# Which loads go around one DMA engine: two of q in place of three of k

## The chip, the core, the metric

One NeuronCore of a Trainium2 chip; the time is the device time of one execution in microseconds (us). A ratio is the mean time of one kernel's runs over the mean of the other's from the same rounds on the same chip, so it is not quite the ratio of the medians quoted beside it.

## The reference

Rotary embedding of q and k, then all scores per head. Everything is float32.

```python
# batch, seq, heads, dim = 16, 512, 16, 64
q_rot = concat([q1*cos - q2*sin, q1*sin + q2*cos], -1)      # k_rot likewise
scores = einsum('bshd,bthd->bsht', q_rot, k_rot)            # (16, 512, 16, 512)
```

It reads 2 x 33.6 MB and writes 268.4 MB. Any kernel for it moves 336 MB.

## The kernel before

The work runs in 64 steps of 128 rows of one batch (16 batches x 4). In each step TensorE makes 16 score blocks, ScalarE (ACT) copies them from PSUM into one of three 4 MB stage buffers, and SyncE (SP) stores the stage. VectorE (DVE) makes the rotary embedding, TensorE transposes. All loads and stores of q, k and the scores are issued by SP and stand in one queue (q1 on the page: 16992 packets, 329.65 of the 335.87 MB), in the order of their issue (a q load issued at 135.40 us behind three stores has its packets from 156 us), except for the loads named in `RELIEVED`:

```python
RELIEVED = {("k", 5): 0, ("k", 9): 1, ("k", 13): 2}     # (tensor, batch): number
SLOW = 4

def load(which, b):
    ...                                                  # buffers: two of q, two of k, by b % 2
    if (which, b) not in RELIEVED:
        dma(SP, ..., dram[which][b], sem, writes=rows + rest)          # 2 MB, 128 rows
        return
    n, E, F = 120, C * H * D, C * H * D // 2
    x = RELIEVED[which, b]
    plan.add(POOL, None, (), rows)                       # wait until the buffer is free, then
                                                         # reset the cursor of GpSimd's DMAs
    ...                                                  # 5 tiny rows (SLOW + 1) ahead of the load
    dma(POOL, nc.gpsimd, dst, src, "cursor", ...)
    ...                                                  # rows 0..119, each in two halves of 8 KB
    dma(POOL, nc.gpsimd, dst, src, f"part{x}", writes=rows)
    dma(SP, nc.sync, t[n:]..., d[n:], sem, writes=rest)  # rows 120..127
```

In the trace of this kernel each relieved load is 240 packets of 8 KB, 16 (8 rows) on each of 15 of the 16 sequences of packets; the sequence left out is the slow one. With six tiny rows in place of five (around5 below) another one was left out, one that stores at 1213 ns elsewhere. No record carries the number of an engine: the engine left out with five tiny rows is called engine 4 here. The loop over steps ends with

```python
    if i % C == C - 2:
        load("q", i // C + 2)     # in SP's order: behind the store of this step
    elif i % C == C - 1:
        load("k", i // C + 3)
```

Of the kernel before, what the change touches and what calls it, by code (L numbers as in the profile page):

```python
# [178 lines left out]
def kernel(  # L179
# [56 lines left out]
    def dma(engine, e, dst, src, sem, reads=(), writes=(), also=()):  # L236
        plan.add(engine, one(lambda: e.dma_start(dst, src)), reads, writes, sem=sem, also=also)  # L237
# [19 lines left out]
            writes=[("unit", which, u) for u in us], also=[x for u in us for x in unit_keys(which, u)],  # L257
        )

    RELIEVED = {("k", 5): 0, ("k", 9): 1, ("k", 13): 2}  # L260
    SLOW = 4

    def load(which, b):
# [5 lines left out]
        rest = [("in rest", which, b % 2, c) for c in range(C)]  # L269
        if (which, b) not in RELIEVED:  # L270
            dma(SP, nc.sync, t.rearrange("p c (h d) -> p c h d", h=H), dram[which][b], sem, writes=rows + rest)
# [4 lines left out]
        n, E, F = 120, C * H * D, C * H * D // 2  # L276
        x = RELIEVED[which, b]
        plan.add(POOL, None, (), rows)
# [252 lines left out]
```

## Time and profile before

| | before |
|---|---|
| median of its runs | 806.99 us (804.74 to 807.4) |
| span of the profiled run | 803.3 us |
| DMA queues busy | 97.0% + 2.3% |
| PE, ACT, DVE busy | 85%, 70%, 68% |

The page's first part and its account of the DMA issues (tensor moved, issuing engine, count, KB each, median us from issue to landing) show the parties. The lines that carry the argument stand in the prediction below.

```profile
PE 680.6 (85%) x3072; PEld 295.1 (37%) x3072; DVE 544.8 (68%) x516; ACT 562.1 (70%) x647; POOL 4.8 (1%) x12
...
out_dram<-st SPq DMA_DIRECT2D x60, 4096.0 KB, 24.7
q_sb<-in_q_dram SPq DMA_DIRECT2D x15, 2048.0 KB, 27.6
k_sb<-in_k_dram SPq DMA_DIRECT2D x12, 2048.0 KB, 27.1
...
k_sb<-in_k_dram POOLq DMA_DIRECT2D x3, 1920.0 KB, 29.8
```

A 4 MB store moves in 9.7 us (128 packets of 1213 ns over 16 engines) and lands 24.7 us after its issue (the median of 60), so as a rule two or more stand in the queue.

Some words for what follows. q1 is the DMA queue of SP, q0 that of GpSimd. A relief is one load that goes around the slow engine. A deal is the way in which the rows of a transfer are shared out over the engines. A packet is stretched when it takes longer than its nominal time, the one that most packets of its size show (in the kernel before, within 6 ns, 1213 ns for 7180 of 7680 stores of 32 KB and 611 for 2937 of 3480 reads of 16 KB).

### The profile page before, as it was taken

How to read it: one execution, taken by the hardware profiler on the slowest of the kernel's cores; microseconds unless marked ns; L12 is line 12 of the kernel's file. 1: busy time of each engine (PE TensorE's matmuls, PEld its weight loads, DVE VectorE, ACT ScalarE, POOL GpSimd, SP SyncE). 2: the span in 40 equal slices, each digit the busy share in tenths (PEclk: the TensorE clock that was granted, in tenths of full speed). 3: DMA queues.
4: the chain of work that ended last, by engine and by line, in shares of the span. 5: the costliest groups of instructions: out<-in, count | busy, mean ns of one | idle time of the engine just before them, and what ended most of it. 6: DMA issues, size and time to landing. Idle time of an engine off the chain costs nothing.

```text
span 803.3 us, 8192 instructions
## 1 busy us (share of the span) xinstructions
PE 680.6 (85%) x3072; PEld 295.1 (37%) x3072; DVE 544.8 (68%) x516; ACT 562.1 (70%) x647; POOL 4.8 (1%) x12
## 2 busy tenths in 40 slices
PE   4989998968989979795897997979499799799960
PEld 2444443423433334242343443434244344343420
DVE  6999987665866767575686675858478568586400
ACT  3878886757858758673785886768388578578770
POOL 0000000000000000000000000000000000000000
PEclk9999999898999989998899899989889889899995
DMA  8999999999999999999999999999999999999996
GB/s 342 425 423 426 433 425 433 401 370 430 434 433 426 439 429 431 433 381 374 434 429 432 430 432 436 428 437 368 401 423 433 431 433 435 432 435 429 434 432 295
DMA packets 18209, 335.87 MB, mean 418 GB/s; under 512 B 1960, under 2 KB 3240, under 8 KB 4264
## 3 DMA queue, kind: packets, MB, share of 16 engines
q1 hardware_dynamic: 16992, 329.65, 97.0%
q0 software_dynamic: 912, 5.90, 2.3%
q10 hardware_dynamic: 288, 0.13, 0.1%
q8 instruction: 6, 0.10, 0.0%
q14 instruction: 11, 0.09, 0.0%
HBM read 67.24 MB, written 268.44 MB: 418 GB/s over the span
## 4 chain that ended last, share of the span: by engine, by line
DMA 48%; PE 35%; DVE 8%; ACT 5%; issue 1%; ACTq 0%; DVEq 0%; SPq 0%
DMA out_dram<-st 47%; PE ps L393 27%; PE bank L344 9%; ACT st L402 5%; DVE st L319 3%; DVE part L319 2%; DVE k_sb L319 2%; DVE q_sb L319 1%; DMA st<-in_k_dram 1%; DVE kT L362 0%; DVE qT L362 0%; ACTq L110 0%; DVEq L110 0%; SPq L526 0%; SPq L497 0%
## 5 line engine op out<-in xcount | busy, mean ns | idle before, releaser
L402 ACT COPY st<-ps 128x1024 f32<-128x1024 f32 x512 | 495.2, 1018 | 203.6 <-DMA out_dram<-st 109.2
L393 PE MATMUL ps<-kT,qT 64*128 64x512 f32 x2048 | 539.1, 643 | 81.8 <-ACT st L402 81.7
L393 PEld LDWEIGHTS ps<-kT,qT 64*128 64x128 f32 x2048 | 181.7, 194 | 268.7 <-issue 135.1
L362 DVE COPY qT<-bank 128x512 f32<-128x512 f32 x118 | 81.5, 690 | 197.4 <-PE bank L344 197.4
L344 PEld LDWEIGHTS bank<-ident,q_sb 128*128 128x128 f32 x480 | 54.7, 150 | 101.6 <-issue 97.3
L344 PE MATMUL bank<-ident,q_sb 128*128 128x128 f32 x480 | 85.5, 305 | 1.0 <-DVE q_sb L319 1.0
L344 PEld LDWEIGHTS bank<-ident,k_sb 128*128 128x128 f32 x480 | 50.5, 141 | 93.3 <-DVE k_sb L319 44.4
L319 DVE TENSOR_TENSOR part<-q_sb,ss_t 128x1024 f32<-128x1024 f32 x60 | 73.5, 1224 | 10.3 <-DMA q_sb<-in_q_dram 7.6
L344 PE MATMUL bank<-ident,k_sb 128*128 128x128 f32 x480 | 78.7, 287 | 1.6 <-DVE qT L362 0.8
L362 ACT COPY kT<-bank 128x512 f32<-128x512 f32 x122 | 72.6, 598 | 6.7 <-PE bank L344 6.7
L319 DVE TENSOR_TENSOR k_sb<-k_sb,cos_t 128x1024 f32<-128x1024 f32 x60 | 73.5, 1225 | 2.0
L319 DVE TENSOR_TENSOR q_sb<-q_sb,cos_t 128x1024 f32<-128x1024 f32 x60 | 73.5, 1225 | 2.1
L319 DVE TENSOR_TENSOR k_sb<-k_sb,part 128x1024 f32<-128x1024 f32 x60 | 73.5, 1225 | 2.1
L319 DVE TENSOR_TENSOR part<-k_sb,ss_t 128x1024 f32<-128x1024 f32 x60 | 72.9, 1215 | 0.3
L319 DVE TENSOR_TENSOR q_sb<-q_sb,part 128x1024 f32<-128x1024 f32 x60 | 72.9, 1215 | 0.0
L344 PE MATMUL bank<-ident,st 128*128 128x128 f32 x64 | 10.8, 318 | 13.0 <-DVE st L319 12.9
L344 PEld LDWEIGHTS bank<-ident,st 128*128 128x128 f32 x64 | 8.2, 161 | 18.4 <-DVE st L319 16.6
L319 DVE TENSOR_TENSOR part<-st,ss_t 128x1024 f32<-128x1024 f32 x8 | 9.8, 1222 | 6.1 <-DMA st<-in_k_dram 5.7
L319 DVE TENSOR_TENSOR st<-st,part 128x512 f32<-128x512 f32 x16 | 11.0, 690 | 0.5
L319 DVE TENSOR_TENSOR st<-st,cos_t 128x1024 f32<-128x1024 f32 x8 | 9.8, 1225 | 0.3
L362 ACT COPY qT<-bank 128x512 f32<-128x512 f32 x10 | 5.7, 617 | 3.5 <-PE bank L344 3.5
L237 POOL DMA_DIRECT2D scratch<-in_q_dram x3 | 1.8, 616 | 543.2 <-PE bank L344 543.2
(11 smaller groups left out, 9.1 us busy)
## 6 DMA issues: line engine op xcount, KB each, us to landing
out_dram<-st SPq DMA_DIRECT2D x60, 4096.0 KB, 24.7
q_sb<-in_q_dram SPq DMA_DIRECT2D x15, 2048.0 KB, 27.6
k_sb<-in_k_dram SPq DMA_DIRECT2D x12, 2048.0 KB, 27.1
out_dram<-st SPq DMA_DIRECT2D x16, 1024.0 KB, 13.7
k_sb<-in_k_dram POOLq DMA_DIRECT2D x3, 1920.0 KB, 29.8
st<-in_k_dram SPq DMA_DIRECT2D x1, 1536.0 KB, 8.9
st<-in_q_dram SPq DMA_DIRECT2D x1, 1536.0 KB, 12.1
st<-in_k_dram SPq DMA_DIRECT2D x1, 512.0 KB, 4.7
```

Source lines behind the costliest of these rows:

```text
L237: plan.add(engine, one(lambda: e.dma_start(dst, src)), reads, writes, sem=sem, also=also)
L319: plan.add(DVE, one(lambda: nc.vector.tensor_tensor(o, a, b, op=op)), reads, writes, also=more)
L344: done = [nc.tensor.transpose(bank[:, x, :], srcs[x], ident) for x in range(4)]
L362: plan.add(engine, one(lambda: copy(out=dst, in_=src)), [("bank", m)], keys)
L393: nc.tensor.matmul(out=ps[:, r, :], lhsT=lhs[lo:hi, :], rhs=rhs[lo:hi, :], start=True, stop=True)
L402: plan.add(ACT, one(lambda: nc.scalar.copy(out=so, in_=si)), [("ps", y)], [("st", s, p)])
```

## The change

Its intent: relieve engine 4 with loads of q, which become free to start at another moment, and with two instead of three.

```diff
-    RELIEVED = {("k", 5): 0, ("k", 9): 1, ("k", 13): 2}
+    RELIEVED = {("q", 6): 0, ("q", 12): 1}
```

## The prediction

> **What bounds the kernel now.** I read first the page's rows by slice, then its DMA queues, then the chain of waits, then stretches of time, then the single packets of the trace. Slices, queues and chain, from the page:
>
> ```profile
> DMA  8999999999999999999999999999999999999996
> GB/s 342 425 423 426 433 425 433 401 370 430 434 433 426 439 429 431 433 381 374 434 429 432 430 432 436 428 437 368 401 423 433 431 433 435 432 435 429 434 432 295
> ...
> q1 hardware_dynamic: 16992, 329.65, 97.0%
> q0 software_dynamic: 912, 5.90, 2.3%
> ...
> DMA 48%; PE 35%; DVE 8%; ACT 5%; issue 1%; ACTq 0%; DVEq 0%; SPq 0%
> DMA out_dram<-st 47%; PE ps L393 27%; PE bank L344 9%; ACT st L402 5%; DVE st L319 3%; DVE part L319 2%; DVE k_sb L319 2%; DVE q_sb L319 1%; DMA st<-in_k_dram 1%; DVE kT L362 0%; DVE qT L362 0%; ACTq L110 0%; DVEq L110 0%; SPq L526 0%; SPq L497 0%
> ```
>
> The DMA row is full in all inner slices, and the longest single item of the chain is a store of the output. PE is 85% busy, but waits for stage buffers that stores hold. So the bytes bound it: 335.87 MB. A 32 KB store packet takes 1213 ns (7180 of 7680 packets are within 6 ns of that), so 16 engines at full pace move 432 GB/s. The GB/s row is there in most slices and falls in three places, slices 7-8, 17-18 and 27-28 of 20 us. Stretches inside these dips and beside them (us, busy time of the engines, granted clock, DMA share, GB/s):
>
> ```profile
> 120.00:150.00 30.00, 26.26 (x114) 11.21 (x112) 21.50 (x21) 20.82 (x25) 0.00 (x0) 0.89 0.99 427
> 157.00:167.00 10.00, 10.00 (x52) 4.41 (x50) 8.53 (x9) 8.69 (x10) 0.00 (x0) 1.00 1.01 280
> 170.00:178.00 8.00, 4.60 (x22) 1.79 (x20) 4.59 (x5) 2.15 (x3) 0.00 (x0) 0.97 1.01 431
> 355.00:366.00 11.00, 11.00 (x54) 4.63 (x50) 9.53 (x9) 9.31 (x11) 0.00 (x0) 1.00 1.00 268
> 555.00:566.00 11.00, 11.00 (x56) 5.15 (x56) 9.49 (x10) 9.67 (x12) 0.00 (x0) 1.00 1.02 282
> ```
>
> Packets are always in flight (share 1.0), but at 157-167 they move 280 GB/s. What runs there is told by the issues, GpSimd's and SyncE's:
>
> ```profile
> 150.37 0.68 POOL L237 DMA_DIRECT2D scratch<-in_q_dram  x1 [148.85 <-PE bank L344]
> 151.04 0.75 POOL L237 DMA_DIRECT2D k_sb<-in_k_dram  x1
> 348.52 0.58 POOL L237 DMA_DIRECT2D scratch<-in_q_dram  x1 [196.73 <-PE bank L344]
> 349.11 0.75 POOL L237 DMA_DIRECT2D k_sb<-in_k_dram  x1
> ```
> ```profile
> 114.98 20.37 SPq L237 DMA_DIRECT2D out_dram<-st  x3
> 135.40 0.90 SPq L237 DMA_DIRECT2D q_sb<-in_q_dram  x1
> 151.76 0.33 SPq L237 DMA_DIRECT2D out_dram<-st  x1
> ```
>
> The GpSimd load of k (q0) has packets from 156.4 to 178.3 us. The q load that SyncE issued at 135.4 stands in q1 behind three stores and has its 16 KB packets from 156 to 169. Where both loads run, packets stretch: q's from 611 ns to about 1000, q0's 8 KB ones from 309 to about 500. From 170 on q0 runs beside stores and both are at their nominal 309 and 1213. So **a load beside a load costs; a load beside a store does not.** Time over nominal of all packets, divided by 16, is 4.25, 5.04 and 4.68 us for the three relieved loads: 14.0 of 16.6 us in the whole run.
>
> **The slow engine.** Packet records carry no engine number, but following each packet from the end of the one before gives 16 sequences. In one of them the store packets take 1250 ns (427 such packets, evenly spread from 80 to 781 us) and 16 KB reads 620-625: 3% slow. In the windows I followed it is just this sequence that has no q0 packets. So the detour works on the right engine. Its reads beside the k loads stretch too: eight took 8.26 us in the first window and 8.35 in the third, against 5.0 at its own pace, +3.3 us each.
>
> [...] 240 8 KB packets per load, 16 on each of 15 sequences, none on the slow one. [...] 1213, 309, 1213, 309 in a sequence. [...] Here there is one slow sequence, and it is slow long before and after any software DMA. [...]
>
> **The change part by part.** The order of instructions of PE, DVE and ACT is the same in both programs; GpSimd issues two relieved loads in place of three, SyncE's entries keep their places with other sizes. The bytes are the same.
>
> *Removed: three k loads by q0.* The stretch goes: 14.0 us for the mean engine, 3 x 3.3 = 9.9 us for the slow one.
>
> *Added: two q loads by q0. Do they meet another load?* The k buffer comes free at the transposes near a step's end, 10 us after the step's stage buffer landed (139.9 to 150.2), when an SP load of q is just coming up. The q buffer comes free at the second q transpose in the middle of a step. For batch 6 that is step 18: the store that it waits for lands at 227.06, the transposes end at 230.8. q0's first data came 5.4 us after its issue (151.04 to 156.41), so here at about 237. The SP load before it, k of batch 6, stands directly behind that store in q1 and landed on all engines between 227.6 and 231.9. The next one, k of batch 7, stands behind four more stores (9.7 us each), after 275; q0 takes some 24 us beside stores (16 packets of 309, each after a 1213), so it is over by 262. Clear by 5 us in front and over 10 behind. Batch 12 repeats it 24 steps later. Cost of the stretch: near 0 (q0 beside stores: about 0.1 us).
>
> *Moved: bytes of the slow engine.* A relieved load spares it seven of eight 16 KB reads (one of the remaining eight rows is its own): 7 x 0.625 = 4.4 us. Three become two: +4.4 us. [...]
>
> *Sum.* Slow engine: last packet now 798.1, minus 9.9, plus 4.4 = 792.6. The others: mean end now 797.6, the latest 800.7; minus about 14 gives 784 to 787. So the end passes to the slow engine and comes 800.7 - 792.6 = 8.1 us earlier. Time: 806.99 - 8.1 = 798.9, about **799 us** (-1.0%).
>
> **Rivals.** *A: the q loads meet a load after all* (descriptors late, or the order in q1 shifts). Then two stretches stay: slow engine 798.1 - 3.3 + 4.4 = 799.2, the others 800.7 - 4.7; the time is about 805. For it: 5 us is not much. Against: both ends of the gap hang on the same landing, so they shift together. *B: the slow engine matters less without the profiler.* Then the others set the end, near 787: time about 793. Against: the run with profile took 805.04, among the plain ones. *C: the slow engine's lag blocks the stage buffers.* It grows 1.4 us a batch (32 store packets of 37 ns and 16 reads of some 12 ns over nominal): from about 1 us at 75 us, ten batches less the first relief's 4.4 make some 10 us before batch 12; a store lives 22 to 28 us in q1, so it starves only engines that are ahead anyway, not itself. If worse, some us. *D: the change only undoes relief:* with the stretch taken as harmless it is +4.4, 811. Against: the dips in GB/s, and batches with a relieved k load: k issues lie 52.0 and 54.2 us apart across these, about 48.4 elsewhere. *E: another bound.* PE, ACT and DVE keep their order and wait for stores now; no speed below 790 comes from them.
>
> **Range and chances.** Main line 799, A 805, B 793, D 811: 8 in 10 for 794 to 804.5. Faster by over 2% needs less than 790.9, less than B gives: 0.03. Slower by over 2% needs 823: nothing seen leads there, 0.02. Within 2%: 0.95.
>
> **What would show it.** In the changed profile: no dips near 360 and 560, at most small ones near 235-262 and 525-555; the packets there at 309 beside 1213; total time over nominal near 3 us per engine, not 16.6; the span near 795; the last store's sixteen arrivals with one straggler about 5 us or more behind the rest, where now they spread evenly over 6.7 us; GpSimd's two issues some 4 us after a store lands. It is wrong if a 16 KB read of 1000 ns stands beside q0 (A), if the last arrivals bunch (B), or if DMA's share falls below 0.97 in the middle (C).

## The result, and the profile after

| | before | after |
|---|---|---|
| median of its runs (beside each other) | 805.91 us (n 4) | 801.61 us (n 4, 801.0 to 802.06) |
| span of the profiled run | 803.3 us | 799.2 us |
| ratio, 95% interval | | 0.9945 (0.9923 to 0.9967) |

It is 0.55% faster, within 2%, and inside the range of 794 to 804.5; the point, 799 or -1.0%, was 2.6 us too low. The gain was about half of the 8.1 us that the sum gave: 4.4 us by the ratio. The page of the changed kernel, slices, queues and chain:

```profile
DMA  8999999999999999999999999999999999999994
GB/s 346 421 422 424 428 432 427 427 436 430 431 428 431 411 431 426 439 430 433 432 426 433 431 427 431 431 425 420 430 426 436 433 429 434 431 434 403 441 423 180
...
q1 hardware_dynamic: 17120, 331.62, 97.3%
q0 software_dynamic: 608, 3.93, 1.2%
...
DMA 47%; PE 36%; DVE 8%; ACT 6%; issue 1%; ACTq 0%; DVEq 0%; SPq 0%
```

The three dips are gone (370, 374 and 368 GB/s before). The same stretches of time as before, and the two in which the q loads run (columns as in the prediction; the last is GB/s):

```profile
157.00:167.00 10.00, 10.00 (x50) 4.43 (x48) 8.53 (x9) 8.67 (x11) 0.00 (x0) 1.00 1.02 433
230.00:262.00 32.00, 28.64 (x122) 11.90 (x120) 20.98 (x20) 22.07 (x26) 0.00 (x0) 0.89 1.01 429
522.00:556.00 34.00, 29.94 (x120) 12.41 (x120) 20.30 (x20) 23.49 (x27) 1.33 (x2) 0.85 1.01 423
355.00:366.00 11.00, 11.00 (x53) 4.68 (x52) 9.49 (x10) 9.67 (x12) 0.00 (x0) 1.00 1.01 435
```

433 where it was 280, 435 where it was 268, and 429 and 423 beside the new GpSimd loads. Those loads are issued as foreseen, in the timeline of GpSimd, and between two SP loads, in that of SyncE:

```profile
228.14 0.69 POOL L237 DMA_DIRECT2D scratch<-in_q_dram  x1 [226.62 <-PE bank L344]
228.82 0.75 POOL L237 DMA_DIRECT2D q_sb<-in_q_dram  x1
526.51 0.58 POOL L237 DMA_DIRECT2D scratch<-in_q_dram  x1 [296.94 <-PE bank L344]
527.09 0.75 POOL L237 DMA_DIRECT2D q_sb<-in_q_dram  x1
```
```profile
201.07 1.03 SPq L237 DMA_DIRECT2D k_sb<-in_k_dram  x1
210.72 24.33 SPq L237 DMA_DIRECT2D out_dram<-st  x3
235.09 1.12 SPq L237 DMA_DIRECT2D q_sb<-in_q_dram  x1
251.17 0.35 SPq L237 DMA_DIRECT2D out_dram<-st  x1
251.56 1.38 SPq L237 DMA_DIRECT2D k_sb<-in_k_dram  x1
```

The k load issued at 201.07 had landed by 228.85; q0's packets run from 234.5 to 257.2; the next k load came after. Nothing overlaps here. In the second window six 16 KB reads, of the eight rows that SP loads itself, ran beside the last 5 us of q0, at 612 to 968 ns. The end is told by the sixteen arrivals of the last store, one from each engine (from the records of its semaphore, us):

```
          first    median   15th     last
before    794.28   798.11   800.48   801.01
after     787.06   787.20   790.01   796.96
```

Before, the arrivals spread over 6.7 us; after, fifteen end 11 us earlier at the median and one straggles by 7. That it is the slow engine shows in its pace: the straggler's last nine stores arrive at 718.04, 727.99, 737.98, 747.94, 757.88, 767.79, 777.61, 787.28 and 796.96, that is 9.8 to 10.0 us each (about 1250 ns a packet) up to about 777 and 9.68 after.

### The profile page after: what moved, and what is told of

The parts are those of the page before. It is cut to its first block, busy times and chain, and to the rows that moved or that the text cites.

```text
span 799.2 us, 8189 instructions
## 1 busy us (share of the span) xinstructions
PE 686.3 (86%) x3072; PEld 297.0 (37%) x3072; DVE 545.2 (68%) x516; ACT 562.5 (70%) x647; POOL 3.5 (0%) x10
## 4 chain that ended last, share of the span: by engine, by line
DMA 47%; PE 36%; DVE 8%; ACT 6%; issue 1%; ACTq 0%; DVEq 0%; SPq 0%
DMA out_dram<-st 47%; PE ps L393 27%; PE bank L344 9%; ACT st L402 6%; DVE st L319 3%; DVE part L319 2%; DVE k_sb L319 2%; DVE q_sb L319 1%; DMA sin_t<-in_sin_dram 0%; DVE kT L362 0%; DVE qT L362 0%; ACTq L237 0%; ACT ss_t L439 0%; ACT ss_t L438 0%; ACTq L110 0%
## 5 line engine op out<-in xcount | busy, mean ns | idle before, releaser
L362 DVE COPY kT<-bank 128x512 f32<-128x512 f32 x6 | 4.1, 683 | 0.0
```

The costliest lines, as they stand in the source:

```text
L362: plan.add(engine, one(lambda: copy(out=dst, in_=src)), [("bank", m)], keys)
```

## The experiments

Eleven other kernels ran, and the changed one once more. All gave right results. First the ledger, from each profiled run: the last packet of the straggler and the median engine's (for the kernel before the slow engine is not the last; its own end is given). GpSimd loads go around engine 4 if nothing else is said. The rounds ran on different chips, so runs of different rounds are better compared by their ratios.

```
                         median time   ratio to before   slow engine's  median engine's
                         us                              last packet    last packet
none                     804.98        1.001             799.3          791.2
k x3 (before)            804.7-805.2   1                 798.1          797.8 (latest 800.7)
k x2                     802.01        0.9987            797.5          790.5
k x3, delayed            800.12        0.9957            795.1          787.2
q x2 (the change)        802.58        0.9963            797.1          789.0
q x3                     800.17        0.9945            795.5          787.9
q x4                     798.62        0.9923            794.1          787.8
q x5                     799.07        0.9918            794.0          788.3
q x6                     798.47        0.9922            not last       791.0 (latest 793.5)
q x2, only 60 rows       803.02        0.9961            801.1          792.8
q x2, around engine 5    806.51        1.002             800.8          791.2
q x2, all 16 engines     805.32        1.0007            799.9          790.4
k x3, all 16 engines     806.14        1.0011            802.7          793.3
```

Theory: **the slow engine sets the end; the old k loads also stretched everybody's packets because they met a load of q; the q loads do not.** Rivals: the number of GpSimd loads is what costs; the tensor k is; any GpSimd load would do; any engine may be left out.

### No relief, and two of k

```diff
-    RELIEVED = {("q", 6): 0, ("q", 12): 1}
+    RELIEVED = {}                              # none
+    RELIEVED = {("k", 6): 0, ("k", 12): 1}     # k2
```

> No load goes by GpSimd; all by SyncE. My theory after the result: the slow DMA engine sets the end, and each of the two q reliefs saved it 4.4 us of reads but cost it about 2.2 us because its stores ran at 1500 ns and not 1250 while the other engines mixed q0 packets into theirs. Then without any relief the time is about 801.6 + 2 x 2.2 = 806, the last store's straggler about 13 us or more behind the rest, and no store packet of 1500 ns in a row. As I predicted before (relief worth its full 4.4 us): 810. If relief is worth nothing: 801.6.

> Two k loads (batches 6 and 12) by GpSimd: the count of the change, the tensor of the kernel before. My theory: reads stretch beside q loads in two places, slow engine 798.1 + 4.4 - 3.3 = 799.2 at its last packet, time about 806 to 807; two dips to 280 GB/s. Rival count: 801.6 as the changed kernel.

Without relief: 804.98 us, ratio 1.001 (0.9991 to 1.0028). So **the three k reliefs of the kernel before were worth nothing that can be measured**: they moved the slow engine's end from 799.3 to 798.1 and the median engine's from 791.2 to 797.8. My 806 was near, but the straggler's last store came 8.2 us behind the median, not 13; the 810 that goes with a full 4.4 us per relief is out.

Two of k: 802.01 us, ratio 0.9987 (0.9956 to 1.0019; one of its six runs took 809.89, which the ratio feels and the median does not), and not 806 to 807. Part of that miss is my own sum: 799.2 at the last packet means 803.5 to 805.5 and no more (at the kernel before, the span is 2.6 us and the time 4.3 to 6.3 us over the last packet). The rest is that the slow engine ended at 797.5, 1.7 us better than by my step. The dips are there in the stretches of the two loads, the second shallower than the 280 GB/s that I foresaw:

```profile
205.00:215.00 10.00, 10.00 (x50) 4.41 (x52) 8.53 (x9) 8.67 (x11) 0.00 (x0) 1.00 1.02 301
500.00:512.00 12.00, 12.00 (x60) 5.25 (x59) 9.84 (x11) 10.22 (x12) 0.00 (x0) 1.00 1.02 369
```

The time alone fits the rival "count" (it said 801.6), so this run does not decide between count and kind. Indeed at two loads the kinds are nearly level: by the medians two of k are at 0.9967 of the kernel before (802.01 over 804.68), two of q at 0.9947 (801.61 over 805.91) and 0.9970 (802.58 over 805.01, below). So the changed kernel's gain may come in large part from having one k load fewer; no run here separates the two. What the kind is worth shows at three loads, in the next two runs.

### Three of q; three of k, delayed

```diff
-    RELIEVED = {("q", 6): 0, ("q", 12): 1}
+    RELIEVED = {("q", 5): 0, ("q", 9): 1, ("q", 13): 2}     # q3
```
```diff
 # k3late, against the kernel before: GpSimd also waits for the landing of the q load ahead
-        plan.add(POOL, None, (), rows)
+        plan.add(POOL, None, [("in", "q", (b - 1) % 2, c) for c in range(C)], rows)
```

> Three q loads (batches 5, 9, 13) by GpSimd, as many as the kernel before has of k. Same count as before, other kind: tells kind from count. My theory: another 4.4 - 2.2 us from the slow engine, time about 799.5. As predicted at first (no cost beside stores): 797. Rival, that the count of three GpSimd loads is what costs (not which tensor): about 806, as before, with dips in GB/s at all three.

> The kernel before (k of batches 5, 9, 13 by GpSimd around the slow engine), but GpSimd waits until the q load that SyncE issued before has landed, so that the two loads no longer overlap. Theory (the overlap of two loads is what stretched the packets, not the tensor): no stretch of 16 KB reads to 1000 ns, no dips, the slow engine ends at 798.1 - 9.9 + about 2.4 x 3 (its stores stretched beside q0 as with the q loads) = 795.4, time about 800, as with three q loads. Rival (it is the k load itself, whenever it runs): dips stay, time about 804.7, as before. A later k load may also hold up DVE for some us; that would show as DVE waiting for k_sb.

Three of q: 800.17 us, ratio 0.9945 (0.9932 to 0.9958). Three loads as before, and 4.5 us faster: the count alone is not what costs. Three of k that wait: 800.12 us, ratio 0.9957 (0.9925 to 0.9988; one run of six took 807.81). The same k loads, only 15 us later, give what three of q give: it is not the tensor. Issue of the first in the timeline of this kernel, and stretches before, at the place of the old overlap, and where the load now runs:

```profile
165.58 0.69 POOL L237 DMA_DIRECT2D scratch<-in_q_dram  x1 [164.07 <-PE bank L344]
166.26 0.75 POOL L237 DMA_DIRECT2D k_sb<-in_k_dram  x1
```
```profile
120.00:150.00 30.00, 26.10 (x120) 11.19 (x118) 21.55 (x20) 21.39 (x25) 0.00 (x0) 0.94 0.99 424
157.00:167.00 10.00, 10.00 (x50) 4.43 (x48) 8.53 (x9) 8.67 (x11) 1.42 (x2) 1.00 1.00 428
172.00:190.00 18.00, 15.37 (x60) 6.12 (x58) 10.30 (x11) 9.99 (x12) 0.00 (x0) 0.81 1.02 432
```

428 and 432 GB/s, against 280. **The overlap with another load is the cause of the stretch**, and the two kernels come to it from both sides.

### The same k loads over all 16 engines

```diff
 # against the kernel before
-        n, E, F = 120, C * H * D, C * H * D // 2
+        n, E, F = 128, C * H * D, C * H * D // 2
         ...                                        # and neither the cursor's load nor SP's rest
```

> The kernel before, but the three k loads go by GpSimd with all 128 rows over all 16 engines, with no detour and no rest by SyncE; still beside the q load. Tells the cause of the stretch. [...] with 128 rows both loads are dealt alike, so no stretch: q reads at 611 and q0 packets at 309, no dips, time about 805, as with no GpSimd load. Rival queues (two reading queues on one engine, or reads from HBM, cost by themselves): stretch and dips stay, and the slow engine has them on top of its full load: 805 + 3 x 4.7 = 819.

806.14 us, ratio 1.0011 (0.9998 to 1.0025). The load of k still lies on that of q: from 157 to 165 us both queues have packets. The stretch is gone. Of 88 reads of 16 KB that start between 158 and 164 none is over 615 ns, and 105 q0 packets take 311 ns in the mean; in the kernel before it was about 1000 and 500. Stretches of this kernel, then of the kernel before:

```profile
157.00:165.00 8.00, 8.00 (x41) 3.63 (x40) 6.94 (x7) 7.19 (x9) 0.00 (x0) 1.00 1.01 432
```
```profile
157.00:165.00 8.00, 8.00 (x42) 3.42 (x38) 7.21 (x7) 7.13 (x9) 0.00 (x0) 1.00 1.00 280
```

Here two loads at once are harmless when both have 128 rows (432 GB/s). So it is not two reading queues, nor HBM as such; it is **the deal of 120 rows over 15 engines beside that of 128 rows** (280 GB/s). Why these two slow each other is not shown.

### GpSimd without detour; detour around another engine

```diff
 # q128, against the changed kernel: n = 128 as above, no cursor, no rest
 # around5, against the changed kernel
-    SLOW = 4
+    SLOW = 5
```

> The changed kernel, but its two q loads go by GpSimd over all 16 engines, with no detour: a GpSimd load without relief. Theory: nothing is saved on the slow engine, time about 805, as with no GpSimd load at all; and since no engine is left out, no engine has a row of 1500 ns stores. Rival (a GpSimd load between two loads of SyncE is itself of use, for instance because it is issued earlier): 801.6.

> The changed kernel with the cursor one row further: the detour leaves out engine 5 and not 4. Theory: the slow engine keeps its full load [...]: 806, straggler 13 us or so. The rows of 1500 ns stores should move to the engine that is left out if it is the leaving out that makes them; if they belong to the slow engine they vanish or stay with it. Rival (any engine may be left out): 801.6.

q128: 805.32 us, ratio 1.0007 (0.9987 to 1.0028), as without GpSimd, and the slow engine's last packet at 799.9 against 799.3: the issuing engine brings nothing by itself. around5 (six tiny rows in place of five): 806.51 us, ratio 1.002 (1.0005 to 1.0035), one straggler at 800.8 with all others near 791. So it must be engine 4, on this chip too; the runs were on several chips, and a detour around 4 helped on each (0.9945 on chip 6 in q3, 0.9957 on chip 0 in k3late, 0.9963 on chip 7 in after2).

around5 also answers a question that the changed kernel had raised. There, beside q0, one sequence of packets has stores of 1376, 1501, 1558, 1473, 1473, 1498, 1500, 1518 and 1528 ns, one directly behind the other from 242.0 to 255.5 us. An engine that takes part in q0 has a 309 ns packet between its stores; this one has none, so it is the engine left out, the slow one, and it lost 2.2 us against its own 1250 ns. Short packets mark it as well: the engine left out has q0 packets of 4 bytes in turn with these stores (at 242.022, 243.401 and 244.913 us, for instance). By them it can be followed in the second window too: 1492, 1469, 1539, 1300, 1674 and 1314 ns from 543.45 to 552.27 us, 1.3 us over 1250 each. In around5 a sequence of stores without 309 ns packets has 1413, 1509, 1478, 1446, 1465, 1491, 1468, 1476 and 1380 ns from 242.65 to 255.9: the same picture on engine 5, which otherwise stores at 1213. In q128, whose load is not sent around any engine, no store between 235 and 262 us is over 1290 ns. **Being left out of the GpSimd load costs that engine's stores up to 2.2 us a load**, often less: 2.2, 1.4 and 0.7 us in the three of q3. The first delayed k load shows it too (ten stores of 1292 to 1528 ns from 178.5 to 193 us). The 4-byte packets are not what slows the stores: in the second load of around5 all of them had passed by 537.4 us, and the stores that follow on that engine, end to start, took 1267, then 1442, 1433, 1424, 1427, 1407 and 1438 ns. This is what the prediction had at near 0.

### Which rows GpSimd takes

```diff
 # q64, against the changed kernel: GpSimd loads rows 64..123, SP rows 0..63 and 124..127
-        n, E, F = 120, C * H * D, C * H * D // 2
+        n, E, F, lo = 60, C * H * D, C * H * D // 2, 64
+        ...                                            # SP: t[:64] <- d[:64]; t[124:] <- d[124:]
```

> The changed kernel, but GpSimd loads only rows 64 to 123 of q (60 rows, 15 engines, 4 rows each, still around the slow engine); SyncE loads rows 0 to 63 and 124 to 127. Aimed at the 1500 ns stores of the engine that is left out. [...] its stores stay at 1250 beside q0, and stores of other engines stretch instead. Rival (being left out makes it, whatever the rows): its stores go to 1500 again, for about half as long. Relief is 2.5 us a load and not 4.4: from the 805 without relief, time about 801 if the stores stay at 1250, about 803 if they stretch.

803.02 us, ratio 0.9961 (0.994 to 0.9983). With q0 in flight from 234.7 to 246.7 us, no store at all between 225 and 256 us is over 1290 ns: the engine left out is not slowed in this window. But in the full load its slow stores came only 7.5 us after q0 began, and q0 is half as long here. In the second load, with q0 from 534.5 to 547.0 us, the engine that has the 4-byte packets does have slow stores, 1315, 1446, 1400 and 1291 ns from 538.96 to 544.45 us (six other engines have one slow store each, near 539 us). So the two loads disagree, and the run does not show that the rows matter: why an engine that is left out is slowed stays open.

The run shows something else instead. SP's load of rows 0 to 63 is slow: in its middle its 16 KB reads take about 1280 ns (1115 in the mean from 256 to 262 us), up to 2.1 times the 611 of a 128-row load. Stretches of this kernel beside q0, then in that load:

```profile
234.00:246.00 12.00, 7.47 (x28) 3.09 (x26) 4.46 (x5) 4.15 (x5) 0.00 (x0) 0.72 1.00 428
256.00:262.00 6.00, 6.00 (x32) 2.54 (x28) 5.86 (x6) 5.19 (x7) 0.00 (x0) 1.00 0.99 273
```

273 GB/s with nothing but these 64 rows and stores; why is not shown. This load also spoils the time (803, which I had expected if the stores stretch) as a measure: the load in halves brings its own stretch.

### How many

```diff
+    RELIEVED = {("q", 5): 0, ("q", 8): 1, ("q", 11): 2, ("q", 14): 3}                                 # q4
+    RELIEVED = {("q", 4): 0, ("q", 6): 1, ("q", 9): 2, ("q", 11): 3, ("q", 14): 4}                    # q5
+    RELIEVED = {("q", 4): 0, ("q", 6): 1, ("q", 8): 2, ("q", 10): 3, ("q", 12): 4, ("q", 14): 5}      # q6
```

> The changed kernel once more, unaltered, on this chip, so that four and five q reliefs can be compared with it: 0.994 to 0.996 of the kernel before, about 801.5, with rows of about 1500 ns stores on the engine left out beside both q loads.

> Four q loads (batches 5, 8, 11, 14) by GpSimd. The slow engine gained 1.3 us per relief from none to three (799.3 to 795.5 at its last packet): with four it ends at 794.2, time about 799. The others end near 789 and do not set the time.

> Five q loads (batches 4, 6, 9, 11, 14). Slow engine at about 793, the others at 791 to 793: about the balance, time 797 to 798.5. With six it was 798.5, and there the others were last. Rival: no further gain after three, 800.

> Six q loads (batches 4, 6, ..., 14) by GpSimd. My theory: the slow engine ends 4 x 2.2 = 9 us earlier than with two, at about 788; the others end near 787 + 4 x 0.7 = 790; both meet, time about 794 to 796. As predicted at first: others bound, 793. Rival count: each GpSimd load costs every engine a few us, time over 806.

The changed kernel again: 802.58 us, 0.9963 (0.994 to 0.9985). Four: 798.62 us, 0.9923 (0.9898 to 0.9948). Five: 799.07 us, 0.9918 (0.9897 to 0.9939), a little over the 797 to 798.5 that I expected. Six, on another chip: 798.47 us, 0.9922 (0.9909 to 0.9935), not the 794 to 796 that I expected. With six the last store's arrivals run from 785.87 to 793.77, and the latest nine stores arrive every 9.68 us: the end has passed from the slow engine to engines at full pace. From four on it is a plateau. **Four or five loads of q beat both kernels**: 0.8% under the kernel before, and 0.4% under the changed one (799.47 us mean of six runs against 802.65, same rounds).

From none to four the slow engine's last packet moves from 799.3 to 794.1, 1.3 us per relief, of the 4.4 us of reads that each one saves it. The slower stores (0.7 to 2.2 us a load in the loads followed above) cover only part of the difference; the rest is not explained.

## Why the prediction was right, and where it was off

- *The bytes bound it, and the slow engine and the others have to be counted apart*: right. Every run's time follows its latest engine.
- *A load beside a load costs; a load beside a store does not*: right for the fifteen engines (432 GB/s beside q0 in k3late, 429 and 423 in the changed kernel). Its first half needs a rider: only where 120 rows met 128 (280 GB/s), not 128 beside 128 (432, k128).
- *The q loads meet no other load*: right, but for six reads at the end of the second. I put q0's first data at about 237 and its end by 262; they were 234.5 and 257.2. The front gap was 5.6 us, as estimated at 5. So rival A is out.
- *The others end at 784 to 787*: about right, 786.7 to 789.6, 786.8 at the median.
- *The slow engine ends at 792.6*: **this is the term that was off; it ended at 796.5.** The step that failed is "Cost of the stretch: near 0 (q0 beside stores: about 0.1 us)". I read it from the mean of all stores beside q0, at 170 to 178 us, where the engine left out indeed kept its 1250 ns. Beside the q loads its stores took about 1500. In the first window that is 2.2 us by nine packets, in the second 1.3 us by six. 3.5 us are thus accounted for, of 3.9. Counted from the run without relief the miss is larger: 799.3 less twice 4.4 is 790.5, against 796.5 measured, and 2.5 us of that are not explained. around5 and q128 show that leaving out makes it. Why it begins only some time after q0 starts (7.5 and 11.0 us here, 6.4 to 16.2 in q3), and why it did not appear beside the k loads of the kernel before, stays open. The fall of the end was therefore 4.2 us and not 8.1; that the time still fell inside the range is owed to the range's width, which reached nearly to the 805 of rival A, and not to the sum.
- *The stretch of the slow engine, 3 x 3.3*: a little low. Its eight reads in the second window, which the sum did not look at, took 8.76 us, so +3.8 there. And that engine is not quite without q0 packets: it has those of 4 bytes.
- *Time over nominal near 3 us per engine*: it was 6.0 (16.6 before). The kernel without any GpSimd load has 8.2, so this is not from the change: some ordinary loads stretch as well, one of k after 269 us by 0.85 us per engine.
- *One straggler, 5 us or more behind*: right, 7.0. With it rival B is out: the slow engine sets the end, and no run of the changed kernel comes near 793.
- *Rival C, the lag blocks the stage buffers*: it came late and did no harm. Between 715 and 735 us the share falls to 0.96. The idle time lies on the fast engines, for the straggler keeps its pace of 10 us a store through it.

```profile
715.00:735.00 20.00, 18.33 (x90) 7.72 (x87) 14.32 (x14) 15.55 (x19) 0.00 (x0) 1.00 0.96 411
690.00:710.00 20.00, 20.00 (x98) 8.84 (x96) 15.74 (x16) 17.07 (x20) 0.00 (x0) 0.99 1.02 437
```

- *Rival D, the change only undoes relief* (811): out. Undoing all of it costs nothing against the kernel before (1.001).

## What to carry to other kernels

When DMA is busy all the time, look for GB/s that falls while the busy share stays full (280 for 432 at a share of 1.0 here), and ask which two transfers are in flight there; moving one of them by 15 us gained 0.4% here, where three reliefs without that had gained nothing. In these runs a transfer that took a detour was better placed beside stores (432 GB/s in k3late) than beside a load that was dealt over the engines in another way (280). And a cost read as a mean over sixteen engines can be near zero while the one engine that sets the end pays it in full: read the critical engine's own packets, and in the place where the new transfer will run.
